# The first two modulation vectors read in units of two row blocks, scale before shift

## The chip, the cores and the metric

The kernel runs on one core of a Trainium2 chip. The metric is the device time of one execution, in microseconds (us). Five engines work side by side, each through its own queue in order: TensorE (PE: matrix products; PEld: its weight loads), VectorE (DVE), ScalarE (ACT), GpSimd (POOL) and SyncE (SP), which here issues nearly all DMA transfers.

## The reference, cut to what matters

Two decoder layers over 256 tokens of width 1024: a gated-linear-attention mixer (GLA) with a dense feed-forward, then an attention mixer with eight experts. Before each part the tokens are normalized, scaled and shifted with vectors computed from a conditioning vector `c`:

```python
cond = jax.nn.silu(c)
mod = (cond @ ada_w[i] + ada_b[i])[:, None, :]
sh1, sc1, g1, sh2, sc2, g2 = jnp.split(mod, 6, axis=-1)
h = rms_norm(x, norm_gain[i, 0]) * (1.0 + sc1) + sh1
mix = gla_mixer(h, ...)
```

`ada_w[0]` is 1024 x 6144 in float32. Its columns 0 to 1023 give the shift of the first norm and columns 1024 to 2047 its scale; with r the reciprocal root mean square of a token, h is x * r * a + s, where a is the gain times (1 + scale) and s is the shift. Only these two vectors and this first norm are touched here.

## The kernel before

All products of the first layer are split: a float32 weight tile `raw` is cast on ScalarE to a rounded high part `whi` (line 224), VectorE subtracts to get the low part `wlo` (line 226), and TensorE adds three products. The activations are split likewise into `h_gla_h` and `h_gla_l`.

Weights come in units of 1 MB into a pool of seven `raw` buffers; `unit` (line 203) issues each transfer on SP's queue, and the order of the queues is set by a scheduler at build time.

The first stage (`with wk.phase("first")`) goes like this. `ada_first` takes eight units, alternately of the scale (`j` = 1) and of the shift (`j` = 0); each has all 1024 rows and 256 columns, so the rows that the DMA moves are 1 KB long. For each unit three of the eight row blocks of 128 (`PE_K` = 3) are multiplied on TensorE (line 279, result `adar`), five on VectorE into `afa` (lines 281 and 283); one further product on TensorE adds `afa` up over the partitions (line 285), ScalarE copies the row out (line 287), two small products turn it into a column (line 291), and VectorE adds the bias and multiplies by the gain (lines 294, 296). Each unit thus finishes a quarter of one vector.

Between these, `during` issues the small transfers and the tokens `xtok` (1 MB), and ScalarE and TensorE make the sums of squares and the transposed tokens `xT`. `Norm.scale` turns the reciprocal root into a 128x256 tile `n_rs_gla` (TensorE, then a VectorE copy, line 400). `Norm.apply` then makes each of eight blocks of h: GpSimd multiplies `xT` by `n_rs_gla` (line 410), ScalarE scales and shifts into `h_gla_h` (line 411), VectorE does the same (line 412) and subtracts (line 413). As a quarter of a and s finishes, two blocks of h can be made.

Then GLA begins. Its first weights are Q (head 0's query and key columns, two transfers of 512 KB with rows of 512 B), V and R, 1 MB each. Their tiles are cast in four parts of 128x512. `qk` are Q's products, `v` and `r` those of V and R; `glow` is a narrow product for the forget gate, copied to `gT` and used by `z`. Three more vectors of ada_w (`ada_gen`, in units of two row blocks x 1024 columns, rows of 4 KB) are mixed in on VectorE (`adacc`, lines 320 and 322).

## Time and profile before

| | us |
|---|---|
| median of 3 runs | 1490.9 |
| lowest, highest | 1485.96, 1493.13 |
| the profiled execution | 1488.84 |
| its span, first to last instruction | 1487.1 |

| engine | busy us | share of the span |
|---|---|---|
| PE | 1411.8 | 95% |
| DVE | 957.3 | 64% |
| ACT | 695.2 | 47% |
| POOL | 80.4 | 5% |

The page gives each engine's busy time over the whole span, which averages stages with different limits. The span cut in 40 slices shows when TensorE was not busy; the stretch views give busy times, the granted clock (1.00 is 2.4 GHz, 0.50 is 1.2 GHz) and the DMA rate of a stage; the chain of waits says what the end was waiting for; the timeline gives single instructions with their start, length and what released them. Times in these views count from the start of the span.

### The profile page before, as it was taken

What the parts mean: (1) busy time and instruction counts of PE and PEld (TensorE: products, weight loads), DVE (VectorE), ACT (ScalarE), POOL (GpSimd) and SP (SyncE); (2) the same over time, 40 slices, a digit from 0 to 9 for tenths busy, and PEclk for the clock granted to TensorE, in tenths of its full rate; (3) what the DMA queues carried; (4) which work ended last, traced back from release to release, by engine and by line L of the source; (5) the groups of instructions that cost most, each with busy time, mean ns of one, the idle gap of its engine ahead of it and who ended that gap; (6) DMA issues with size and microseconds to landing.
All of it is one profiled execution on the core that took longest, in us unless ns stands there. A gap on an engine that the chain in (4) does not pass through costs nothing.

```text
span 1487.1 us, 21658 instructions
## 1 busy us (share of the span) xinstructions
PE 1411.8 (95%) x8443; PEld 1075.4 (72%) x8443; DVE 957.3 (64%) x1292; ACT 695.2 (47%) x984; POOL 80.4 (5%) x87
## 2 busy tenths in 40 slices
PE   6999999999999997999997999997999997999986
PEld 2899999999999997888532788532888433888422
DVE  7786897778987777799410989500989402989201
ACT  3653644335566555687300777301777202777000
POOL 2000200000132024000000000000000000000000
PEclk9999999999999998899999999999999999999998
DMA  9996578898855334699799999999999999999996
GB/s 316 362 337 221 198 267 321 302 327 286 285 169 152 132 114 170 245 348 385 281 411 403 409 408 402 393 409 402 409 408 403 393 408 403 409 406 405 380 406 261
DMA packets 183000, 488.86 MB, mean 329 GB/s; under 512 B 10815, under 2 KB 51913, under 8 KB 182890
## 3 DMA queue, kind: packets, MB, share of 16 engines
q1 hardware_dynamic: 182602, 486.87, 87.8%
q8 instruction: 68, 1.11, 0.3%
q10 hardware_dynamic: 288, 0.52, 0.1%
q14 instruction: 42, 0.34, 0.1%
HBM read 486.32 MB, written 1.05 MB: 328 GB/s over the span
## 4 chain that ended last, share of the span: by engine, by line
PE 84%; DMA 11%; DVE 3%; SPq 1%; issue 0%; ACT 0%; DVEq 0%
PE mo L1258 10%; PE mo L243 7%; PE mo L241 7%; PE mo L242 7%; DMA raw<-in_moe_w_down_dram 6%; PE md L241 4%; PE md L242 4%; PE md L243 3%; PE gu L247 3%; PE gu L249 3%; PE gu L248 3%; PE md L1258 3%; DMA raw<-in_moe_w_gate_dram 3%; PE dn L247 2%; PE dn L248 2%; PE dn L249 2%
## 5 line engine op out<-in xcount | busy, mean ns | idle before, releaser
L226 DVE TENSOR_TENSOR wlo<-raw,whi 128x1024 fp32r<-128x1024 f32 (+2 forms) x481 | 567.7, 1230 | 59.4 <-ACT whi L224 57.6
L224 ACT CAST whi<-raw 128x1024 fp32r<-128x1024 f32 (+2 forms) x491 | 486.2, 1053 | 199.6 <-PE gu L248 67.2
L1258 PE MATMUL mo<-raw,gs 128*64 128x512 f32 (+1 forms) x1024 | 205.6, 543 | 13.4 <-DMA raw<-in_moe_w_up_dram 7.2
L241 PE MATMUL mo<-whi,g 128*128 128x512 f32 x448 | 176.3, 394 | 0.9 <-ACT gf L1145 0.9
L242 PE MATMUL mo<-whi,g 128*128 128x512 f32 x448 | 175.7, 392 | 0.0
L1258 PEld LDWEIGHTS mo<-raw,gs 128*64 128x64 f32 x1024 | 70.3, 137 | 135.0 <-issue 101.2
L1301 DVE TENSOR_TENSOR msg<-msg,mo 128x512 f32<-128x512 f32 (+1 forms) x16 | 9.9, 620 | 218.8 <-PE mo L1258 218.8
L243 PE MATMUL mo<-wlo,g 128*128 128x512 f32 x448 | 148.0, 396 | 0.0
L1258 PE MATMUL md<-raw,gs 128*64 128x512 f32 x448 | 104.3, 600 | 13.6 <-DMA raw<-in_moe_w_down_dram 13.6
L241 PEld LDWEIGHTS mo<-whi,g 128*128 128x128 f32 x448 | 84.8, 189 | 19.8 <-issue 1.1
L243 PEld LDWEIGHTS mo<-wlo,g 128*128 128x128 f32 x448 | 83.7, 189 | 20.1 <-DVE wlo L226 3.5
L242 PEld LDWEIGHTS mo<-whi,g 128*128 128x128 f32 x448 | 84.8, 189 | 17.9
L322 DVE SCALAR_TENSOR_TENSOR adacc<-raw,csil,adacc 128x1024 f32<-128x1024 f32 x70 | 90.0, 1286 | 7.5 <-DMA raw<-in_ada_w_dram 7.1
L1270 ACT COPY gs<-actT 128x512 f32<-128x512 f32 (+1 forms) x16 | 8.5, 533 | 179.8 <-PE md L1258 117.8
L249 PE MATMUL gu<-h_ffn_h,wlo 128*128 128x256 f32 x320 | 90.5, 284 | 0.0
L248 PE MATMUL gu<-h_ffn_l,whi 128*128 128x256 f32 x320 | 90.1, 282 | 0.0
L247 PE MATMUL gu<-h_ffn_h,whi 128*128 128x256 f32 x320 | 89.9, 283 | 0.0
L1258 PEld LDWEIGHTS md<-raw,gs 128*64 128x64 f32 x448 | 29.2, 136 | 80.2 <-issue 48.7
L241 PE MATMUL md<-whi,act_h 128*128 128x512 f32 x192 | 76.0, 396 | 0.0
L242 PE MATMUL md<-whi,act_l 128*128 128x512 f32 x192 | 75.8, 395 | 0.0
L243 PE MATMUL md<-wlo,act_h 128*128 128x512 f32 x192 | 64.0, 400 | 0.0
L248 PE MATMUL dn<-act_l,whi 128*128 128x256 f32 x224 | 62.2, 283 | 0.0
(487 smaller groups left out, 2655.3 us busy)
## 6 DMA issues: line engine op xcount, KB each, us to landing
raw<-in_moe_w_gate_dram SPq DMA_DIRECT2D x112, 1024.0 KB, 14.1
raw<-in_moe_w_up_dram SPq DMA_DIRECT2D x112, 1024.0 KB, 13.8
raw<-in_moe_w_down_dram SPq DMA_DIRECT2D x112, 1024.0 KB, 14.0
raw<-in_ada_w_dram SPq DMA_DIRECT2D x48, 1024.0 KB, 7.0
raw<-in_fox_w_in_dram SPq DMA_DIRECT2D x16, 1024.0 KB, 6.1
raw<-in_ffn_w_gate_dram SPq DMA_DIRECT2D x14, 1024.0 KB, 5.1
raw<-in_ffn_w_up_dram SPq DMA_DIRECT2D x14, 1024.0 KB, 5.8
raw<-in_ffn_w_down_dram SPq DMA_DIRECT2D x14, 1024.0 KB, 5.0
```

What stands on the lines that cost most here:

```text
L224: nc.scalar.copy(hi[:, s], raw[:, s])
L226: (nc.gpsimd if i in pool else nc.vector).tensor_tensor(lo[:, s], raw[:, s], hi[:, s].bitcast(F32), op=ALU.subtract)
L241: nc.tensor.matmul(ps, ah, wh, start=first, stop=False)
L242: nc.tensor.matmul(ps, al, wh, start=False, stop=False)
L243: return nc.tensor.matmul(ps, ah, wl, start=False, stop=last)
L247: i = nc.tensor.matmul(ps, wh, ah, start=first, stop=False)
L248: nc.tensor.matmul(ps, wh, al, start=False, stop=False)
L249: nc.tensor.matmul(ps, wl, ah, start=False, stop=last)
L322: nc.vector.scalar_tensor_tensor(a, raw[:, kk, :], csil[:, k:k + 1], a, op0=ALU.mult, op1=ALU.add)
L1258: nc.tensor.matmul(ps[64 * i:64 * (i + 1), 0:n], a, w[:, i * n:(i + 1) * n], start=first, stop=last)
L1270: nc.scalar.copy(t, pt[:, 0:hw].rearrange("p (q i t) -> p q i t", q=n, i=2))
L1301: nc.vector.tensor_mul(sg, sg, ps[:, 0:hw])
```

## The change

`ada_first` takes its eight units in another shape and order: first the four units of the scale, then the four of the shift, each of two row blocks x 1024 columns, so that the DMA's rows are 4 KB long. Units 0 and 1 hold the row blocks that TensorE multiplies (three blocks, 2 x 512 columns each) and the first one for VectorE; units 1 to 3 hold the five blocks that VectorE accumulates in a 128x1024 tile `adacc`. TensorE's rows are copied out once and turned into columns, VectorE's tile is summed over the partitions by eight one-column products, and both are added to the bias. A vector is complete only after its last unit.

The tokens are loaded behind the scale's last unit. When the shift's first unit is done, `Norm.scale` runs and x * r * a is made for all eight blocks in a tile `ua` (GpSimd, then ScalarE in place). After the shift, ScalarE adds it to give `h_gla_h`, and one VectorE instruction per block gives `h_gla_l`, in place of two. `Norm.apply` is no longer used for this norm.

```diff
--- before.py
+++ after.py
@@ -264,36 +264,39 @@
             nc.vector.tensor_mul(m, m, gain[:, g:g + KD])
 
     def ada_first(mid):
-        js = (1, 0)
-        ps = {j: wk_ps(f"adaps_{j}") for j in js}
-        for j in js:
-            mod[0, j] = cst.tile([P, KD], F32, name=f"mod_0_{j}")
-        for u in range(4):
-            for j in js:
-                c0 = j * D + u * 256
-                raw = unit([(ada_w[0][:, c0:c0 + 256], lambda v: v)], KD)
-                rp = acc_ps(f"adar_{j}_{u}")[0:1, 0:256]
-                acc = wk.tile([P, 256], F32, tag="afa", name=f"afa_{j}_{u}")
-                for k in range(KD):
+        for j in (1, 0):
+            m = mod[0, j] = cst.tile([P, KD], F32, name=f"mod_0_{j}")
+            a = ada["p"].tile([P, D], F32, tag="adacc", name=f"adacc_0_{j}", bufs=2)
+            rp = [acc_ps(f"adar_{j}_{h}")[0:1, :] for h in range(2)]
+            ps = wk_ps(f"adat_0_{j}")
+            for u in range(4):
+                raw = unit([(ada_w[0][u * 2 * P:(u + 1) * 2 * P, j * D:(j + 1) * D], lambda v: v)], 2)
+                for kk in range(2):
+                    k = 2 * u + kk
                     if k < PE_K:
-                        nc.tensor.matmul(rp, csil[:, k:k + 1], raw[:, k, :], start=(k == 0), stop=False)
+                        for h in range(2):
+                            nc.tensor.matmul(rp[h], csil[:, k:k + 1], raw[:, kk, h * 512:(h + 1) * 512], start=(k == 0),
+                                             stop=(k == PE_K - 1))
                     elif k == PE_K:
-                        nc.vector.tensor_scalar(acc, raw[:, k, :], csil[:, k:k + 1], None, op0=ALU.mult)
+                        nc.vector.tensor_scalar(a, raw[:, kk, :], csil[:, k:k + 1], None, op0=ALU.mult)
                     else:
-                        nc.vector.scalar_tensor_tensor(acc, raw[:, k, :], csil[:, k:k + 1], acc, op0=ALU.mult,
-                                                       op1=ALU.add)
-                nc.tensor.matmul(rp, ones[:, 0:1], acc, start=False, stop=True)
-                row = wk.tile([1, 256], F32, tag="afr", name=f"afr_{j}_{u}")
-                nc.scalar.copy(row, rp)
+                        nc.vector.scalar_tensor_tensor(a, raw[:, kk, :], csil[:, k:k + 1], a, op0=ALU.mult, op1=ALU.add)
+                if u == 1:
+
+                    row = wk.tile([1, D], F32, tag="afr", name=f"afr_{j}", bufs=1)
+                    for h in range(2):
+                        nc.scalar.copy(row[:, h * 512:(h + 1) * 512], rp[h])
+                    for k in range(KD):
+                        nc.tensor.matmul(ps[:, KD + k:KD + k + 1], row[:, k * P:(k + 1) * P], ones[0:1, 0:1], start=True,
+                                         stop=True)
                 mid(u, j)
-                s = slice(2 * u, 2 * u + 2)
-                for h in range(2):
-                    nc.tensor.matmul(ps[j][:, 2 * u + h:2 * u + h + 1], row[:, h * P:(h + 1) * P], ones[0:1, 0:1],
-                                     start=True, stop=True)
-                m = mod[0, j][:, s]
-                nc.vector.tensor_add(m, ps[j][:, s], bias[:, j * KD + s.start:j * KD + s.stop])
-                if j == 1:
-                    nc.vector.tensor_mul(m, m, gain[:, s])
+                if u == 2:
+                    nc.vector.tensor_add(m, ps[:, KD:2 * KD], bias[:, j * KD:(j + 1) * KD])
+            for k in range(KD):
+                nc.tensor.matmul(ps[:, k:k + 1], a[:, k * P:(k + 1) * P], ones[:, 0:1], start=True, stop=True)
+            nc.vector.tensor_add(m, m, ps[:, 0:KD])
+            if j == 1:
+                nc.vector.tensor_mul(m, m, gain[:, 0:KD])
 
     def ada_gen(todo):
         def end(i, j, a):
@@ -1448,7 +1451,7 @@
         def during(u, j):
             if (u, j) == (0, 1):
                 load_cols()
-            if (u, j) == (1, 1):
+            if (u, j) == (3, 1):
                 for b in range(NB):
                     ld.dma_start(xtok[:, b, :], x[0, b * P:(b + 1) * P, :])
                     t = wk.tile([P, D], F32, tag="xsq", name=f"xsq_{b}", bufs=1)
@@ -1460,6 +1463,11 @@
                             nc.tensor.transpose(ps[:, k, b * P:(b + 1) * P],
                                                 xtok[:, b, (2 * q + k) * P:(2 * q + k + 1) * P], ident)
                     nc.scalar.copy(xT[:, 2 * q:2 * q + 2, :], ps)
+            if (u, j) == (0, 0):
+                n0.scale(ss0)
+                for k in range(KD):
+                    nc.gpsimd.tensor_tensor(ua[:, k, 0:T], xT[:, k, :], n0.r, op=ALU.mult)
+                    nc.scalar.activation(ua[:, k, 0:T], ua[:, k, 0:T], AF.Copy, scale=mod[0, 1][:, k:k + 1])
             if (u, j) == (1, 0):
                 load_small(glac, "wg_raw", gla_w_in[0], 3072, 16)
                 for i in range(2):
@@ -1469,12 +1477,16 @@
                 for t, v, n in ((bf_c, fox_b_f, 16), (br_c, moe_b_router, E)):
                     ld.dma_start(t, bass.AP(tensor=v.tensor, offset=v.offset, ap=[[1, n], [1, 1]]))
 
+        n0 = Norm("gla", "X", lambda: mod[0, 1], lambda: mod[0, 0])
+        ua = big.tile([P, KD, W], F32, tag="Yh", name="ua")
         ada_first(during)
-        n0 = Norm("gla", "X", lambda: mod[0, 1], lambda: mod[0, 0])
-        n0.scale(ss0)
-        h, step = n0.apply("X")
+        hh, hl = at(pair("X", "h_gla"), A_, A_, slice(0, T))
         for k in range(KD):
-            step(k)
+            sh = mod[0, 0][:, k:k + 1]
+            nc.scalar.activation(hh[:, k, :], ua[:, k, 0:T], AF.Identity, bias=sh)
+            nc.vector.scalar_tensor_tensor(hl[:, k, :], ua[:, k, 0:T], sh, hh[:, k, :].bitcast(F32), op0=ALU.add,
+                                           op1=ALU.subtract)
+        h = hh, hl
     with wk.phase("gla"):
         gen = ada_gen([(0, 2), (0, 4), (0, 3)])
         go, last = gla(h, small["wg_raw"], lambda: next(gen, None))
```

Numbers at the end of a name in the next listings tell buffers apart. On SP's queue, where the last units of ada_w stand ahead of GLA's first weights (128x8x256 is a unit in the old shape or V and R, 128x2x1024 one in the new shape, 128x8x128 half of Q, g_145 the 512 KB tile of a bias row), before:

```order
L1467 DMA wgu<-in_gla_b_gate_dram 1x512
L203 DMA raw<-in_ada_w_dram 128x8x256 x2
L1470 DMA bf_c<-in_fox_b_f_dram 16x1
L1470 DMA br_c<-in_moe_b_router_dram 8x1
L203 DMA raw<-in_ada_w_dram 128x8x256 x2
L203 DMA raw<-in_gla_w_in_dram 128x8x128 x2
L301 DMA g_145<-in_ada_b_dram 128x1024
L203 DMA raw<-in_gla_w_in_dram 128x8x256 x2
L203 DMA raw<-in_ada_w_dram 128x2x1024
```

and now:

```order
L1474 DMA wgu<-in_gla_w_gate_up_dram 16x512 x2
L1475 DMA wgu<-in_gla_b_gate_dram 1x512
L203 DMA raw<-in_ada_w_dram 128x2x1024
L1478 DMA bf_c<-in_fox_b_f_dram 16x1
L1478 DMA br_c<-in_moe_b_router_dram 8x1
L304 DMA g_145<-in_ada_b_dram 128x1024
L203 DMA raw<-in_ada_w_dram 128x2x1024
L203 DMA raw<-in_gla_w_in_dram 128x8x128 x2
L203 DMA raw<-in_gla_w_in_dram 128x8x256 x2
```

The bias tile has moved from behind Q to ahead of the last unit of the shift; V and R follow Q as before.

On VectorE, around the copy of the norm's factor, n_rs_gla (afa and adacc are the sums over row blocks, n_u and h_gla_l the norm's blocks, mod the two vectors), before:

```order
L296 TENSOR_TENSOR mod_1_154<-mod_1_154,cols 128x2
L281 TENSOR_SCALAR afa_1_257<-raw,csil 128x256
L283 SCALAR_TENSOR_TENSOR afa_1_257<-raw,csil,afa_1_257 128x256 x3
L400 COPY n_rs_gla<-n_r_gla 128x256
L283 SCALAR_TENSOR_TENSOR afa_1_257<-raw,csil,afa_1_257 128x256
L281 TENSOR_SCALAR afa_2_280<-raw,csil 128x256
L412 TENSOR_SCALAR n_u_gla_365<-n_u_gla_365,mod_1_154,mod_0_155 128x256
L283 SCALAR_TENSOR_TENSOR afa_2_280<-raw,csil,afa_2_280 128x256
L413 TENSOR_TENSOR h_gla_l<-n_u_gla_365,h_gla_h 128x256
L412 TENSOR_SCALAR n_u_gla_370<-n_u_gla_370,mod_1_154,mod_0_155 128x256
```

and now:

```order
L281 TENSOR_SCALAR adacc_0_243<-raw,csil 128x1024
L283 SCALAR_TENSOR_TENSOR adacc_0_243<-raw,csil,adacc_0_243 128x1024
L403 COPY n_rs_gla<-n_r_gla 128x256
L283 SCALAR_TENSOR_TENSOR adacc_0_243<-raw,csil,adacc_0_243 128x1024 x2
L294 TENSOR_TENSOR mod_0_242<-adat_0_246,bias 128x8
L283 SCALAR_TENSOR_TENSOR adacc_0_243<-raw,csil,adacc_0_243 128x1024
L643 MEMSET gT 33x256
L489 TENSOR_TENSOR wg<-wg_raw,wg 128x8x16
L226 TENSOR_TENSOR wlo<-raw,whi 128x512 x2
L297 TENSOR_TENSOR mod_0_242<-mod_0_242,adat_0_246 128x8
L226 TENSOR_TENSOR wlo<-raw,whi 128x512 x2
L1487 SCALAR_TENSOR_TENSOR h_gla_l<-ua,mod_0_242,h_gla_h 128x256 x8
```

The copy stood after three of the second scale quarter's five small steps; it now stands behind the shift's second 1024-wide step, the first that reads the third unit, and Q's `wlo` stand ahead of all of h_gla_l.

On ScalarE, around the casts of Q's weights (the first four casts to whi), before:

```order
L411 ACTIVATE h_gla_h<-n_u_gla_380,mod_0_155,mod_1_154 128x256
L287 COPY afr_2_290<-adar_2_279 1x256
L287 COPY afr_2_309<-adar_2_298 1x256
L411 ACTIVATE h_gla_h<-n_u_gla_385,mod_0_155,mod_1_154 128x256
L411 ACTIVATE h_gla_h<-n_u_gla_390,mod_0_155,mod_1_154 128x256
L287 COPY afr_3_329<-adar_3_318 1x256
L224 CAST whi<-raw 128x512 x4
L287 COPY afr_3_348<-adar_3_337 1x256
L224 CAST whi<-raw 128x512 x4
L411 ACTIVATE h_gla_h<-n_u_gla_395,mod_0_155,mod_1_154 128x256
L411 ACTIVATE h_gla_h<-n_u_gla_400,mod_0_155,mod_1_154 128x256
L224 CAST whi<-raw 128x512 x4
```

and now:

```order
L288 COPY afr_283<-adar_0_244 1x512
L1470 ACTIVATE ua<-ua,mod_1_154 128x256
L288 COPY afr_283<-adar_1_245 1x512
L1470 ACTIVATE ua<-ua,mod_1_154 128x256 x7
L488 CAST wg<-wg_raw 128x8x16
L224 CAST whi<-raw 128x512 x4
L1486 ACTIVATE h_gla_h<-ua,mod_0_242 128x256 x8
L224 CAST whi<-raw 128x512 x8
```

Six blocks of h_gla_h stood ahead of Q's casts and two behind V's; now eight steps on ua and the cast of wg stand ahead of Q's casts, and all of h_gla_h behind them.

## Rows read from the trace of the kernel before

**Rows 1.** page part 2, 40 slices of the span: TensorE busy tenths, DMA busy tenths

```profile
PE   6999999999999997999997999997999997999986
...
DMA  9996578898855334699799999999999999999996
```

**Rows 2.** busy time of each engine in stretches (x instructions), granted TensorE clock, DMA, GB/s

```profile
0.00:37.00 37.00, 24.55 (x113) 10.90 (x113) 28.51 (x89) 12.28 (x26) 9.82 (x22) 1.00 1.02 316
37.00:45.00 8.00, 7.62 (x44) 6.77 (x44) 4.55 (x12) 4.98 (x11) 0.00 (x0) 0.79 1.08 364
45.00:60.00 15.00, 15.00 (x127) 14.61 (x126) 14.44 (x20) 7.28 (x10) 0.57 (x2) 1.00 1.08 359
60.00:75.00 15.00, 15.00 (x102) 12.70 (x102) 11.37 (x10) 13.55 (x18) 0.00 (x0) 1.00 1.08 362
```

**Rows 3.** chain that ended last, first 120 us: start us, us, what

```profile
22.73 0.63 DVE afa L281
...
38.05 0.61 DVE wlo L226
38.71 0.63 PE qk L249 x2
...
43.34 0.53 PE adaps L291 x4
```

**Rows 4.** DMA from 20 to 31 us, the 1 KB rows

```profile
DMA packets 3915, 3.82 MB, mean 347 GB/s; under 512 B 109, under 2 KB 3915, under 8 KB 3915
```

**Rows 5.** DMA from 700 to 1400 us, the 4 KB rows of the experts

```profile
GB/s 353 348 248 408 410 394 410 408 410 408 409 395 409 408 374 410 408 399 406 409 408 409 408 402 402 409 393 390 410 408 396 409 408 409 409 409 395 409 408 347
DMA packets 78054, 277.63 MB, mean 397 GB/s; under 512 B 4226, under 2 KB 4226, under 8 KB 78012
```

**Rows 6.** timeline: start us, us, engine line op out<-in xcount [idle before <-releaser]

```profile
18.97 0.35 DVE L281 TENSOR_SCALAR afa<-raw,csil 128x256 f32<-128x256 f32 x1 [0.73 <-DMA raw<-in_ada_w_dram]
...
21.12 0.42 DVE L400 COPY n_rs_gla<-n_r_gla 128x256 f32<-128x256 f32 x1 [0.24 <-PE n_r_gla L397]
21.46 0.47 DVE L283 SCALAR_TENSOR_TENSOR afa<-raw,csil,afa 128x256 f32<-128x256 f32 x1
21.69 2.24 POOL L410 TENSOR_TENSOR n_u_gla<-xT,n_rs_gla 128x256 f32<-128x256 f32 x3 [3.89 <-DVE n_rs_gla L400]
...
22.73 0.63 DVE L281 TENSOR_SCALAR afa<-raw,csil 128x256 f32<-128x256 f32 x1 [0.79 <-DMA raw<-in_ada_w_dram]
...
25.06 0.94 DVE L283 SCALAR_TENSOR_TENSOR afa<-raw,csil,afa 128x256 f32<-128x256 f32 x1
...
25.78 1.46 PE L279 MATMUL adar<-raw,csil 128*1 128x256 f32 x6 [1.05 <-DMA raw<-in_ada_w_dram]
...
29.38 2.11 POOL L410 TENSOR_TENSOR n_u_gla<-xT,n_rs_gla 128x256 f32<-128x256 f32 x2 [2.00 <-DVE h_gla_l L413]
...
36.42 2.18 ACT L224 CAST whi<-raw 128x512 fp32r<-128x512 f32 x4 [0.36 <-DMA raw<-in_gla_w_in_dram]
...
37.09 0.38 PE L247 MATMUL qk<-h_gla_h,whi 128*128 128x256 f32 x1 [0.38 <-ACT whi L224]
```

**Rows 7.** groups of instructions, 0 to 50 us: busy us, mean ns, idle before

```profile
L283 DVE SCALAR_TENSOR_TENSOR afa<-raw,csil,afa 128x256 f32<-128x256 f32 x32 | 16.7, 523 | 0.6
...
L410 POOL TENSOR_TENSOR n_u_gla<-xT,n_rs_gla 128x256 f32<-128x256 f32 x8 | 6.8, 870 | 12.3 <-DVE h_gla_l L413 8.4 <-DVE n_rs_gla L400 3.9
...
L411 ACT ACTIVATE h_gla_h<-n_u_gla,mod,mod 128x256 fp32r<-128x256 f32 x8 | 4.5, 595 | 7.6 <-DVE mod L294 4.6 <-POOL n_u_gla L410 3.0
...
L485 ACT CAST wg<-wg_raw 128x128 fp32r<-128x128 f32 x1 | 0.3, 304 | 1.2 <-DVE h_gla_l L413 1.2
```

**Rows 8.** the same view, VectorE, 40 to 200 us

```profile
L322 DVE SCALAR_TENSOR_TENSOR adacc<-raw,csil,adacc 128x1024 f32<-128x1024 f32 x26 | 33.2, 1277 | 0.2
```

**Rows 9.** TensorE busy (x instructions), its granted clock, DMA, GB/s in stretches

```profile
39.00:42.00 3.00, 3.00 (x16) 0.50 1.11 359
...
585.00:606.00 21.00, 14.86 (x54) 0.51 0.57 214
```

## The prediction, made before the changed kernel was run

> **What bounds the kernel now.** I read the 40 slices first. TensorE is busy 9 tenths or more almost everywhere but in the first slice, and the DMA is at 9 through the first five slices [rows 1]. The edited stage lies in the first 45 us, so I went to the stretches. From 0 to 37 us TensorE is busy 24.55 us and the DMA's share is 1.02; from 45 us on TensorE is busy 15.00 us of every 15, with 127 instructions in the first such stretch, that is 0.118 us for a product of 256 columns [rows 2]. So TensorE sets the time from about 39 us on, and what the first stage is worth is read from one moment: when GLA's products first run without a gap. An earlier such moment moves all that follows, since later transfers are issued as `raw` buffers come free.
>
> The chain of waits gives the moment. It runs through a first-stage step on VectorE at 22.73 that waited for its unit, through VectorE's steps up to Q's first `wlo` at 38.05, and from 38.71 through TensorE [rows 3]. The first product of Q came at 37.09 behind a cast that had waited for Q's transfer until 36.42 [rows 6]. Four products ran before the gap that ended at 38.71 (4 x 0.118 = 0.47), and 0.53 us of the old stage's column products still came later, at 43.34 [rows 3]. The moment to compare with is therefore 38.71 - 0.47 + 0.53 = **38.8 us**. DMA and VectorE were nearly level there: Q landed at about 36.4, VectorE's last steps ended at 38.
>
> **The change part by part: the transfers.** A unit of 1.049 MB with 1 KB rows moves at 347 GB/s, 3.02 us [rows 4]; the trace has 22.73 to 25.78 between two landings [rows 6]. The experts' 4 KB rows hold 408 to 410 GB/s in most slices, 397 in the mean [rows 5]: 2.57 us a unit (2.64 by the mean). I take 2.57, since the tokens behind the scale are 4 KB rows too and nothing else shares the queue: 0.45 us saved a unit, 3.6 on eight. A unit's content is the same, so no other transfer pays.
>
> The Trainium skill, page "DMA: Bandwidth & Descriptors", section Specifications, gives 512 B as the smallest transfer at line rate, by which 1 KB rows would already be at full speed and the edit would save nothing. The rows above disagree, 347 against 408 GB/s, and I go by them; what the other reading would give is the third rival.
>
> The third unit of the shift is seventh of eight. The sixth landed at 25.78 before, so the seventh now lands at 25.78 + 3.02 - 7 x 0.45 = **25.7 us**. The bias tile (0.52 MB, 1.3 us at 408 GB/s) now goes ahead of the eighth: 25.7 + 1.3 + 2.6 = 29.6. Q, seen at 36.42, comes 3.6 earlier and 1.3 later: **34.1 us**.
>
> **VectorE's sums and the shift.** Before, the stage had 32 steps of 523 ns in `afa` [rows 7] and two norm steps a block. Now it has eight 1024-wide steps of 1.28 us [rows 8], two shorter ones, and one norm step a block. That is some 10 us less, most of which buys nothing: VectorE waits for units (idle 0.73 and 0.79 us ahead of two of them [rows 6]). What counts is the order. The copy of `n_rs_gla` stands behind the shift's second 1024-wide step, which needs the seventh unit: 25.7 + 1.28 + 0.42 for the copy [rows 6] = 27.4 us. Before, that copy was made at 21.12 [rows 6]. So all eight GpSimd products, made in pieces behind the old stage, now begin at 27.5 us, although x and its norm are there long before.
>
> **GpSimd, where I have to choose.** Three of them took 2.24 us, 0.75 each, with VectorE mostly idle [rows 6]: eight take 6.0 and end at 33.5. But three VectorE steps of 1.28 us, with two tile inputs, run in the same stretch. Where they met before, a 0.47 us VectorE step took 0.94 and GpSimd's pair took 2.11, 1.05 each [rows 6]; the mean of all eight is 870 ns [rows 7]. The upper bound is that GpSimd stands for the whole of each: 6.0 + 3 x 1.28 = 9.8, ending at 37.3. The 0.47 that VectorE's step grew by is most of one GpSimd product, so the rows lie near the upper end, and I take 36.9.
>
> The page "SBUF — State Buffer" of the Trainium skill, section "SBUF: two separate sides", says that a VectorE instruction with two SBUF inputs and a GpSimd one that reads SBUF exclude each other for a whole instruction. By that the end would be the upper bound, by the free row alone the lower; the lengthened rows agree with it in kind.
>
> **ScalarE and TensorE behind it.** ScalarE follows GpSimd with its last step on `ua` (0.60 [rows 7]), then the cast of wg (0.30), then the four casts of Q (2.18 [rows 6]), then the first `h_gla_h` (0.60). From 33.5 that gives 37.2 for the first product, from 37.3 it gives 41.0. Q's landing at 34.1 is covered in both. `h_gla_l` needs the fourth `wlo`, 0.6 behind the casts (0.61 [rows 3]), and one step of 0.5 [rows 7]: the fourth product starts 0.5 us behind the first, with 0.35 us of work between, so the moment is 37.4 to 41.2. After that ScalarE gives a block each 0.6 us, VectorE one each 0.5, and TensorE needs 8 products, 0.94 us, for it: no further gap. The shift itself is early: eighth unit 29.6, two steps and 16 one-column products, about 34 even with GpSimd's delays.
>
> So the DMA's 3.6 us are saved, and the edit puts GpSimd's eight products, ScalarE's eight and Q's casts in one row behind the seventh unit, which takes 3.6 us or more of them back. **Sum**: 37.4 - 38.8 = -1.4 at best, 41.2 - 38.8 = +2.4 at worst, taken **+2.0**.
>
> **Into GLA.** TensorE's `z` now stands behind 14 of V's products and waits for the copy of `gT`, which stands on VectorE behind eight `h_gla_l`, seven `wlo` and one 1024-wide step: 41.6 + 8 x 0.5 + 7 x 0.61 + 1.28 + 0.4 = 51.6. TensorE gets there at 41.2 + 78 x 0.118 = 50.4, with the low clock that followed its start before (0.50 for 3 us [rows 9], 1.5 us) 51.9. Cover is 0.3 us; without it V's other 34 products wait as well, for at most about 1 us. VectorE is busy 14.44 of 15 us there and 11.37 in the next stretch [rows 2], so a delay is made up. I cost it at nothing, bounds 0 and 1.
>
> Against the profiled execution's 1488.8 the sum gives 1490.8. That run lies 2.1 below the median of 1490.9, from which it would be 1492.9. I put the forecast between, **1492 us**. A measurement here tells 0.5%, 7.5 us, from no change.
>
> **The rivals.** *First, the saving arrives.* GpSimd isn't held up, so Q's products start at 37.4; or VectorE's copy comes sooner than I think because the third unit does. If the full 3.6 came through, the end would be 1488.8 - 3.6 = 1485.2; with -1.4 it is 1487.4. For it: the first three products at 0.75. Against it: ScalarE's and GpSimd's row alone takes 9.7 us from 27.5.
>
> *Second, slower, by TensorE's clock.* TensorE's work before GLA shrinks in the stretch from 27 to 41 us to 2 row blocks and some 30 small products, where before it had products every few us. At its start before, the granted clock stood at 0.50 for about 3 us [rows 9] and was 1.00 again from 45 [rows 2]. At 585 us it stood at 0.51 for 21 us [rows 9]. Were it so low here, each us would cost 0.5: 21 us cost 10.5, less the 1.5 paid already, 9.0, and with +2.0 the end is 1488.8 + 11.0 = 1499.8. It decides from 14 us of low clock on (0.5 x 14 - 1.5 + 2.0 = 7.5). Against it: once products came densely at 39 us, they got their clock back in 3 us.
>
> *Third, the new shape doesn't do what it says:* units with 4 KB rows move no faster here, so the seventh unit lands at 28.8 and everything is 3.1 us later: 1488.8 + 2.0 + 3.1 = 1493.9. Against it: 408 GB/s over 700 us [rows 5].
>
> *Fourth, the new order in GLA* makes TensorE wait for `gT` or the casts: +1 to +4 on the sum, 1492 to 1495.
>
> **How the numbers follow.** Forecast 0.47, first rival 0.20, second 0.12, third 0.06, fourth 0.15. The runs before spread over 7.2 us, so I add some 2 to 3 us at either end. From 1485 (first rival in full) to 1499 (most of the second) leaves out about 0.1 above and 0.07 below. Nearly all cases lie within 7.5 us of before: faster 0.04 (first rival with a good draw), same 0.85, slower 0.11 (most of the second, a piece of the fourth).
>
> **What would show it.** On VectorE, the copy of `n_rs_gla` near 27.4; on GpSimd, eight products from 27.5 to about 37, some of them over 1 us; on ScalarE, the first cast of Q near 38 with GpSimd or ScalarE's own row, not the DMA, as its releaser; on TensorE, the first `glow` and `qk` near 41. The DMA should show about 400 GB/s from 5 to 26 us where it had 347, and Q's landing near 34. It would be wrong if the copy comes before 25 us, if the eight products take under 7 us, if Q's cast waits for its transfer, or if the time moves while the first `qk` doesn't: then the cause lies behind 45 us, in TensorE's clock or in GLA's order.

## The result, and the profile after

The changed kernel takes 1504.0 us in the median (8 runs, 1496.8 to 1505.0), the kernel before on the same chip 1488.9 (8 runs): a ratio of 1.0091, 95% interval 1.0073 to 1.0109. That is 15 us more, outside the range of 1485 to 1499, and slower by over 0.5%, to which I had given 0.11.

The profiled execution has a span of 1503.1 us, 16.0 more than before. TensorE's granted clock over the span fell from 0.986 to 0.976. The stretches that answer to [rows 2] (columns as there: length, TensorE busy, weight loads, VectorE, ScalarE, GpSimd, granted clock, DMA share, GB/s):

```profile
0.00:37.00 37.00, 26.43 (x95) 13.23 (x95) 17.32 (x44) 10.54 (x19) 8.42 (x19) 0.84 0.97 331
37.00:45.00 8.00, 5.15 (x23) 4.77 (x24) 4.64 (x12) 6.55 (x15) 3.50 (x6) 0.50 1.09 353
45.00:60.00 15.00, 15.00 (x101) 13.25 (x100) 14.76 (x21) 10.35 (x16) 0.00 (x0) 0.88 1.07 372
60.00:75.00 15.00, 14.57 (x102) 12.77 (x101) 12.53 (x14) 12.75 (x20) 0.00 (x0) 1.00 1.08 359
```

VectorE has 11 us less work in the first 37 us, as the edit promised, and TensorE runs at half clock where it ran at full: 0.84 against 1.00 to 37 us, 0.50 against 0.79 to 45, 0.88 against 1.00 to 60. The chain of waits of the changed kernel, in the part that answers to [rows 3] (start us, us, what):

```profile
18.88 3.58 PE adat L296 x16
22.46 2.88 PE x L1463 x13
25.33 4.97 PE adar L278 x8
30.30 0.66 PE n_r_gla L400 x4
30.98 0.44 DVE n_rs_gla L403
...
35.54 4.41 POOL ua L1469 x5
...
40.38 0.28 ACT wg L488
40.67 0.53 ACT whi L224
...
44.24 0.39 PE glow L497
```

From 18.9 to 31 us TensorE itself is the chain: the scale's one-column sums, the tokens' transposes and the shift's first row blocks stand in its queue ahead of the norm's matmul. Then come GpSimd and ScalarE, in the order that I had forecast.

The 16 us sit in two places. The experts' first product with `g`, the tile of their gathered tokens, came at 599.65 us before and at 604.76 now: **5.1 us are lost by then**, all of them ahead of the dense stage, which began at 161.9 and at 167.8. From that product to the last group of `sc`, the products that scatter the experts' results back, it took 877.0 us before and 887.9 now: **10.9 us are lost in the experts**, whose instructions and whose order on each engine the edit does not touch. I had not looked there at all.

The first of these differences holds for the two executions profiled and no further. Three later profiles, of kernels with the start of the kernel before (below: routing later, new places, large tiles lower), began the dense stage at 157.7, 158.8 and 159.2. From 135 to 150 us TensorE's granted clock was 0.77 in the profile of the kernel before and 1.00 in those three. So single executions of one start differ by some 4 us, and the price of the start is better taken from medians of whole times.

At each of three places where a small expert pass ends and the next pair begins, the products now start like this (timeline: start us, us, engine line op out<-in):

```profile
825.98 0.74 PE L1202 MATMUL sc<-yh,ohT 64*128 64x512 f32 x2 [1.44 <-ACT yh L1193]
...
827.69 0.80 PE L241 MATMUL mo<-whi,g 128*128 128x512 f32 x1
828.28 0.63 PE L242 MATMUL mo<-whi,g 128*128 128x512 f32 x1
...
830.39 0.40 PE L241 MATMUL mo<-whi,g 128*128 128x512 f32 x1
```

and in the kernel before like this:

```profile
820.06 0.73 PE L1199 MATMUL sc<-yh,ohT 64*128 64x512 f32 x2 [1.44 <-ACT yh L1190]
...
821.45 0.50 PE L241 MATMUL mo<-whi,g 128*128 128x512 f32 x1
821.78 0.40 PE L242 MATMUL mo<-whi,g 128*128 128x512 f32 x1
```

The same pause of 1.44 us, the same products, but in the changed kernel the granted clock stands at 0.50 for a few us behind it, and a product takes 0.63 us instead of 0.40.

### The profile page after: what moved, and what is told of

The parts are those of the page before. It is cut to its first block, busy times and chain, and to the rows that moved or that the text cites. A ratio compares the mean times of both kernels' runs of the same rounds, so it can differ in the third digit from the quotient of the medians.

```text
span 1503.1 us, 21603 instructions
## 1 busy us (share of the span) xinstructions
PE 1425.5 (95%) x8435; PEld 1082.2 (72%) x8435; DVE 950.1 (63%) x1247; ACT 698.4 (46%) x989; POOL 84.9 (6%) x87
## 4 chain that ended last, share of the span: by engine, by line
PE 83%; DMA 11%; DVE 3%; ACT 1%; issue 1%; POOL 1%; SPq 0%; DVEq 0%; POOLq 0%
PE mo L1261 10%; PE mo L241 7%; PE mo L243 7%; PE mo L242 7%; DMA raw<-in_moe_w_down_dram 6%; PE md L241 4%; PE md L242 4%; PE md L243 3%; PE gu L247 3%; PE gu L249 3%; PE gu L248 3%; DMA raw<-in_moe_w_gate_dram 3%; PE md L1261 3%; PE dn L248 2%; PE dn L247 2%; PE dn L249 2%
## 5 line engine op out<-in xcount | busy, mean ns | idle before, releaser
L241 PE MATMUL mo<-whi,g 128*128 128x512 f32 x448 | 180.5, 403 | 0.9 <-ACT gf L1148 0.9
L242 PE MATMUL mo<-whi,g 128*128 128x512 f32 x448 | 179.0, 400 | 0.0
```

The source lines that it names most:

```text
L241: nc.tensor.matmul(ps, ah, wh, start=first, stop=False)
L242: nc.tensor.matmul(ps, al, wh, start=False, stop=False)
```

## The experiments

**What was open.** For the experts I had two theories at first: C, that the falls of the clock make all of the loss and depend on the moment alone, and D, that something in the changed program does. For the start, B: TensorE's queue, at half clock, holds the norm's copy.

**Moving the experts in time.** The kernel before with two more comparisons in the routing, and the changed kernel with one more:

```diff
             nc.vector.tensor_tensor(gt, lj, li, op=ALU.is_gt)
+            nc.vector.tensor_tensor(gt, lj, li, op=ALU.is_gt)
+            nc.vector.tensor_tensor(gt, lj, li, op=ALU.is_gt)
```

> The kernel before, with one comparison of the routing done three times instead of once, some 2.5 us more on VectorE's chain just ahead of the expert stage; nothing else is touched, and the experts' instructions are the same. Theory C (the 10 us that the change lost in the experts are the fall of TensorE's clock at the three passages from an expert's first pass to the next pair, and whether the clock falls there depends only on the moment at which the short pause of that place comes): moved by 2.4 to 3.1 us the passages of the kernel before should show the fall too, and the time goes up by the 2.5 us and by up to 10 more, to about 1498 to 1502. Rival D (the loss in the experts belongs to the changed code: other buffers, other addresses, another layout): the experts keep their times, and only the delay is added, 1490.5 to 1492.

> The changed kernel, with another comparison of the routing done twice, some 0.7 us more ahead of the experts. Theory C: a shift of 0.4 to 0.8 us takes the passages out of the falls that they show, and the time comes DOWN although work is added, to about 1494 to 1496; it stays if the shift is a little short. Rival D: 1504.0 + 0.7 = about 1504.7.

Measured: the first 1489.9 us (ratio 1.0006, 0.9989 to 1.0023), no fall; the second 1503.5 (1.0098, 1.0067 to 1.0129), all three falls. In the traces, from the first `foxo` (a product of the second layer's attention) to the first `mo`, the delays came to 1.9 and 1.3 us, not to the 2.4 to 3.1 and 0.4 to 0.8 that I had expected. Neither changed the side. C as I had put it, that it makes the whole loss, found no support, though two delays of that size, against starts that differ by some 4 us from execution to execution, could not refute it; D stayed.

**The units alone.** The changed kernel with the norm made behind both vectors again, as in the kernel before:

```diff
-            if (u, j) == (0, 0):
-                n0.scale(ss0)
...
         ada_first(during)
+        n0 = Norm("gla", "X", lambda: mod[0, 1], lambda: mod[0, 0])
+        n0.scale(ss0)
+        h, step = n0.apply("X")
```

> The changed kernel with the second part undone: units of two row blocks x 1024 columns, scale first, then shift, but the first norm made behind both, as before. Theory B (the start is late because the copy of x's norm stands behind the shift's sums in TensorE's queue, which run at half clock): the norm's matmul stands still further back there, the copy comes at some 34 us, and the first product of Q at 41.5 to 44, within 1.5 us of the changed kernel's 43.26: the units alone bring the loss of the start, and the early norm brings nothing back. Rival (the loss is the scaling ahead of the shift, its eight steps on GpSimd and eight on ScalarE): the first product returns to 37 to 39. The time with it: first product's shift against 43.26, and 0 or up to -10 from the experts.

Measured 1496.0 us (1.0058, 1.0040 to 1.0076). The first product of Q came at 40.7, between the two theories' ranges, and the dense stage began at 165.6 against 161.9 before and 167.8 after the whole change. So the units without the early norm bring a loss of their own: 6.8 us by the medians (1496.0 against 1489.1 for the kernel before beside it). And the experts took 877.7 us, as before: what slows them belongs to the other part of the edit, the early norm.

**The norm first.** TensorE's matmuls of the norm ahead of the shift's row blocks, and the copy ahead of VectorE's second step of the shift:

```diff
+                    with after(*(() if j == 1 or k == PE_K else by_r[k < PE_K])):
                         if k < PE_K:
```

> The changed kernel, with the norm's two matmuls ahead of the shift's sums in TensorE's queue and the copy of the norm ahead of the shift's second step in VectorE's. Theory B: the matmul goes at about 25.4 instead of 30.2, the copy at about 26 instead of 31.0, GpSimd's eight products end at 34 to 36 instead of 39.9, ScalarE is free for Q's casts when Q lands (35.1), and the first product of Q comes at 38.5 to 40 instead of 43.26: the stages behind move up by 3 to 4.5 us. Rival (Q's landing or the last unit's sums set the end anyway): the copy is early, and the first product moves by less than 1.5 us. The whole time: theory B 1499.5 to 1501 with the falls in the experts as they are, about 1490 if the shift takes them away.

Measured 1505.4 us (1.0120, 1.0097 to 1.0142), where theory B asked for 1499.5 to 1501. The timeline of this kernel:

```profile
25.66 0.42 DVE L406 COPY n_rs_gla<-n_r_gla 128x256 f32<-128x256 f32 x1 [1.18 <-PE n_r_gla L403]
26.23 8.45 POOL L1472 TENSOR_TENSOR ua<-xT,n_rs_gla 128x256 f32<-128x256 f32 x8 [5.73 <-DVE n_rs_gla L406]
...
35.82 2.18 ACT L224 CAST whi<-raw 128x512 fp32r<-128x512 f32 x4
35.96 1.28 DVE L286 SCALAR_TENSOR_TENSOR adacc<-raw,csil,adacc 128x1024 f32<-128x1024 f32 x1
...
37.30 3.57 PE L299 MATMUL adat<-ones,adacc 128*128 128x1 f32 x16 [1.95 <-DVE adacc L286]
...
41.10 3.30 ACT L1491 ACTIVATE h_gla_h<-ua,mod 128x256 fp32r<-128x256 f32 x8 [0.16 <-DVE mod L300]
41.71 0.39 PE L499 MATMUL glow<-h_gla_h,wg 128*32 128x256 f32 x1 [0.84 <-issue]
```

Copy, GpSimd and ScalarE moved up by some five us each, as theory B said, and the first product by 1.55 only (43.26 to 41.71). A second chain of the same length lay behind the first: the shift's own last sum. Its last step on VectorE stands behind an addition of the bias that waits for TensorE, then come eight one-column products at half clock (sixteen entries in the trace, 3.57 us), and only then can ScalarE shift. B had the first chain right and its worth wrong.

**The places of the tiles.** The experts' groups gave the lead. VectorE adds a finished half of `mo` to `msg`; between two such additions of the large pass TensorE is busy without a gap on a fixed set of products that load blocks of `g` and `act`. Before (the first fence) the stretches are 867.70 - 844.99 = 22.71 and 33.88 us, in the changed kernel (the second) 23.27 and 34.47, and VectorE's wait for `mo` grows from 0.79 to 1.10:

```profile
844.99 1.28 DVE L1344 TENSOR_TENSOR msg<-msg,mo 128x512 f32<-128x512 f32 x2 [1.97 <-PE mo L243]
867.70 1.29 DVE L1344 TENSOR_TENSOR msg<-msg,mo 128x512 f32<-128x512 f32 x2 [0.79 <-PE mo L243]
901.58 1.28 DVE L1344 TENSOR_TENSOR msg<-msg,mo 128x512 f32<-128x512 f32 x2 [0.79 <-PE mo L243]
```

```profile
852.69 1.28 DVE L1347 TENSOR_TENSOR msg<-msg,mo 128x512 f32<-128x512 f32 x2 [2.44 <-PE mo L243]
875.96 1.28 DVE L1347 TENSOR_TENSOR msg<-msg,mo 128x512 f32<-128x512 f32 x2 [1.10 <-PE mo L243]
910.43 1.29 DVE L1347 TENSOR_TENSOR msg<-msg,mo 128x512 f32<-128x512 f32 x2 [1.11 <-PE mo L243]
```

The granted clock is 1.00 in both. The expectations and theory E below call `g` the streamed tile. The rows of the products show that it is the loaded one: each block of 128x128 of `g` goes in as the weight, and 512 columns of `whi` or `wlo` stream past it. Before, then now:

```profile
L241 PEld LDWEIGHTS mo<-whi,g x448: 186/188/329, 599.6 to 1364.0; 128*128 128x128 f32 x150
L241 PE MATMUL mo<-whi,g x448: 387/389/793, 599.6 to 1364.3; 128*128 128x512 f32 x150
```

```profile
L241 PEld LDWEIGHTS mo<-whi,g x448: 187/188/330, 604.8 to 1379.6; 128*128 128x128 f32 x150
L241 PE MATMUL mo<-whi,g x448: 392/398/796, 604.8 to 1379.8; 128*128 128x512 f32 x150
```

(ns: least, median, most.) The load takes 188 ns in both, the product 389 and 398. In the profiles up to here this differs in the three kernels that ask for `ua` first and in none of the others. `ua` is the first tile to ask the pool `big` for the tag `Yh`; with that the pool hands out its five places in another order, and `g`, which uses `Xh`, moves from byte 140864 of each partition to byte 149120. Theory E: the place of this tile decides. Two experiments move the tiles of this pool and nothing else. In the changed kernel, the pair `X` goes ahead of `ua`:

```diff
+        hh, hl = at(pair("X", "h_gla"), A_, A_, slice(0, T))
         ua = big.tile([P, KD, W], F32, tag="Yh", name="ua")
```

> The changed kernel with one line moved up: the pair of tiles for the first norm's result is asked for ahead of ua, so that the pool hands out its places in the order of the kernel before (the tile g of the experts is at byte 140864 of each partition again, not at 149120). Instructions and their order stay. Theory E (the 10 us of the experts come from the place of the tiles: the products that stream g take 232 to 235 ns from start to start in the three kernels with ua asked for first, 227 ns in the three others, and the fall of the clock belongs to it): 227 ns again, no fall at the three passages, 9 to 10.5 us back, 1493 to 1495.5. Theory C (falls by moment alone): the products stay at 232 to 235 ns, or the time stays within 2 us of 1504.

In the kernel before, a tile that nothing uses asks for `Yh` first:

```diff
+        big.tile([P, KD, W], F32, tag="Yh", name="yh_first")
         n0 = Norm("gla", "X", lambda: mod[0, 1], lambda: mod[0, 0])
```

> The kernel before, with one tile asked for ahead that nothing uses, so that the pool's places come in the changed kernel's order (g at byte 149120). No instruction is added or moved. Theory E: the products that stream g take 232 to 235 ns, the passages show falls, and the time goes up by 5 (the products alone) to 10 us (with the falls), to 1494 to 1499.5. Theory C: the time of the kernel before, 1488 to 1490.5.

Measured: the changed kernel with the old places 1494.5 us (1.0041, 1.0027 to 1.0055), 5.4 above the kernel before measured beside it, where the changed kernel stood 15.1 above the one beside it: **9.7 less** by moving one line. The kernel before with the new places took 1497.2 (1.0059, 1.0036 to 1.0081), **8.1 more** by an unused tile; its profiled execution, at 1490.1, was the fastest of five, with its first `mo` at 593.8, 5.8 earlier than in the profile of the kernel before. The additions to `msg` of the first,

```profile
848.91 1.28 DVE L1347 TENSOR_TENSOR msg<-msg,mo 128x512 f32<-128x512 f32 x2 [1.95 <-PE mo L243]
871.62 1.28 DVE L1347 TENSOR_TENSOR msg<-msg,mo 128x512 f32<-128x512 f32 x2 [0.79 <-PE mo L243]
```

and of the second:

```profile
840.14 1.28 DVE L1344 TENSOR_TENSOR msg<-msg,mo 128x512 f32<-128x512 f32 x2 [2.37 <-PE mo L243]
863.43 1.28 DVE L1344 TENSOR_TENSOR msg<-msg,mo 128x512 f32<-128x512 f32 x2 [1.10 <-PE mo L243]
```

22.71 and 23.29: E holds both ways. The pool's other tiles move with `g`, but only products with `g` change their pace. From the start of one product to the next, in the median at granted clock 1.00, those with `g` and `whi` take 227 ns before and with the old places, 233 after the change and with the new places. Those that load `act`, which lies in another pool and stays, take 233 to 234 ns in all four, and pairs of those of the small passes, whose tile `gs` moves too, follow each other at 429 ns in all four. Then two more places, one to learn what about a place matters, one in the hope of a faster kernel. In the changed kernel, `Yl` too goes ahead of the pair:

```diff
         ua = big.tile([P, KD, W], F32, tag="Yh", name="ua")
+        big.tile([P, KD, W], F32, tag="Yl", name="yl_first")
```

> The changed kernel with the places moved once more: g at byte 157376, so again 64 bytes past a multiple of 128, as in the kernel before (140864), where the changed kernel has it on a multiple of 128 (149120). If the place within 128 bytes decides: 227 ns for the products that stream g, and about 1494. If it is the distance to the weights' tiles or the region (further up is slower): 233 ns or more, and 1503 to 1506.

In the kernel before, all four streamed tiles go ahead of `xT`:

```diff
+    for tag in ("Xh", "Yh", "Xl", "Yl"):
+        big.tile([P, KD, T + 2], F32, tag=tag, name="place")
     xT = big.tile([P, KD, T], F32, tag="xT", name="xT")
```

> The kernel before, with nothing but the places of the five large tiles changed: the four that TensorE streams are asked for ahead of xT and lie at bytes 132672 (the one of g and of the dense layer's act_h), 140928, 149184 and 157440, each 8 KB or more lower than in the kernel before, and xT above them. Theory E (of the places tried, g streams at 227 ns at 140864, 232 at 157376, 233 to 235 at 149120; the dense layer's tile h_ffn_h at 116.2 ns at 140864 against 117.5 at 157376): if lower is faster or equal, g stays at 227 ns or less, the gate and up products fall to 116 to 117 ns, and the time is 1485 to 1489, at or below the kernel before. Rival (the pairing with the weights' tiles decides, not the height): some product groups get slower, g at 230 ns or more, 1491 to 1496.

Measured 1502.2 us (2 runs; 1.0088, 1.0059 to 1.0118) and 1485.7 (against 1487.7 for the kernel before beside it; ratio 0.9999, 0.9983 to 1.0016). The first refutes the remainder within 128 bytes. The second runs the products with `g` as fast as before and no faster, and its whole time can't be told from the kernel before. The fourteen profiles side by side:

| kernel | byte of `g` | stretches between additions, us | falls at the three passages | first `mo` to last group of `sc`, us |
|---|---|---|---|---|
| before | 140864 | 22.71, 33.89 | 0 | 877.0 |
| before, routing later | 140864 | 22.69, 33.89 | 0 | 878.0 |
| units alone | 140864 | 22.71, 33.89 | 0 | 877.7 |
| changed, old places | 140864 | 22.71, 33.89 | 0 | 878.0 |
| start again (below) | 140864 | 22.69, 33.89 | 0 | 875.6 |
| old places, 20 products more (below) | 140864 | 22.71, 33.89 | 1 | 879.2 |
| start again, 20 products more (below) | 140864 | 22.71, 33.89 | 0 | 875.6 |
| start again, 8 products more (below) | 140864 | 22.69, 33.87 | 2 | 878.6 |
| before, large tiles lower | 132672 | 22.71, 33.89 | 2 | 878.7 |
| changed, fourth place | 157376 | 23.18, 34.38 | 0 | 883.8 |
| before, new places | 149120 | 23.29, 34.46 | 1 | 884.1 |
| changed | 149120 | 23.27, 34.47 | 3 | 887.9 |
| changed, routing later | 149120 | 23.28, 34.46 | 3 | 888.6 |
| norm first | 149120 | 23.27, 34.46 | 3 | 889.1 |

Without a fall the experts take 875.6 to 878.0 us with `g` at 140864 and 883.8 at 157376. So by estimate the place costs some 6 to 8 us of the 10.9, and the three falls the other 4 to 5 (887.9 to 889.1 against 883.8 and 884.1, with at most one fall). The falls are not tied to the place of `g`: two came at its lowest place, three in the profiles with it at 140864, none at the fourth.

**The start again.** With the old places, and all that the norm-first run had asked for: VectorE's last step of the sum ahead of the bias, ScalarE's eight shifts ahead of the cast of the second weight unit:

```diff
+                    with after(*last_k):
                         nc.vector.tensor_add(m, ps[:, KD:2 * KD], bias[:, j * KD:(j + 1) * KD])
...
+        hold(2, *done)
```

> All that the runs so far ask for: the places of the kernel before (as in the run with the pair asked for first), the norm's matmuls ahead of the shift's sums (as before), and besides VectorE's last step of the shift's sum ahead of its bias and of the gate weights, and ScalarE's eight shifts ahead of the cast of the second weight unit. Theory (in the run with the norm first, the tail of the shift's own sums and the second unit's cast held the first product at 41.9): the last step of the sum at 34 to 34.5 instead of 36.0, the sixteen one-column products end at 38.5 to 39.5, the first product of Q at 39.3 to 40.3; with the experts as in the kernel before 1489 to 1492. Rival (Q's landing at 35.1 and the half clock behind it hold the stage whatever comes first): the first product is early, but the stage ends where it did, 1493 to 1495.

Measured 1495.1 us (1.0037, 1.0021 to 1.0053), no better than the old places alone (1494.5). The first product came at 40.9, later than forecast, because the sums still ran at half clock:

```profile
36.47 3.58 PE L300 MATMUL adat<-ones,adacc 128*128 128x1 f32 x16 [0.26 <-DVE mod L298]
```

**Keeping the clock up.** Theory F: the half clock is what the start costs. TensorE multiplies row blocks that VectorE keeps, too, into a bank that nothing reads, first all five of each vector:

```diff
+                for kk in range(2):
+                    if 2 * u + kk >= PE_K:
+                        for h in range(2):
+                            nc.tensor.matmul(spare, csil[:, 0:1], raw[:, kk, h * 512:(h + 1) * 512], start=True, stop=True)
```

> The run with the pair asked for first (places of the kernel before), and TensorE multiplies, besides its own three row blocks, the five that VectorE keeps, into a bank that nothing reads: twenty products of 512 columns more, spread over the units' landings. Theory F (the units of the change leave TensorE idle between their few products, its clock falls to 0.50 from about 19 to 26 us and 36 to 46 us, and the sums, transposes and Q's first products behind it run at half speed): the first low stretch goes, the sixteen one-column products take some 1.8 us instead of 3.6, the norm's copy comes at 27 to 29 instead of 30 to 31, the first product of Q 2 to 3 us earlier (39.3 to 40.5 against 42.3), and the stages behind move up by as much: 1491 to 1493 against 1494.5. Rival (the start is bound by the transfers and by GpSimd, ScalarE and VectorE): the clock stays up, the first product moves by less than 1 us, 1494 to 1496.

> The run with the whole order of the start changed (norm first, the sum's last step ahead, the shifts ahead of the second weight unit's cast), and the same twenty products more. Theory F: the row's transposes and the sums no longer run at half clock, so the last sum ends near 37 instead of 40.1, and the first product of Q comes at 37.5 to 39 instead of 40.9; with the products at full clock from the start the stage ends some 3 us earlier, 1490 to 1492 against 1495.1. Rival (ScalarE's copies and GpSimd's products pace the tail): the first product stays at 40 to 41 and the time at 1494 to 1496.

Measured 1502.8 us (1.0098, 1.0079 to 1.0118) and 1500.7 (1.0095, 1.0076 to 1.0115), both far off. The clock stayed at 1.00 past 46 us, but I had priced a product of 512 columns by half: the trace has two entries of some 0.44 us for each. Of the first kernel:

```profile
27.17 1.84 PE L301 MATMUL adat<-ones,adacc 128*128 128x1 f32 x16
...
35.21 8.75 PE L288 MATMUL spare<-raw,csil 128*1 128x512 f32 x20
```

The added products themselves stood ahead of the last sums for 8.75 us. What these runs give is the price of the sums at full clock, 1.84 us instead of 3.58. The last run adds only what fits into the gaps:

```diff
+                    if (j, 2 * u + kk) in ((1, 3), (1, 4), (0, 4), (0, 6)):
```

> The run with the whole order of the start changed, and only four row blocks more on TensorE (two of the scale, two of the shift, eight products of 512 columns in all, into a bank that nothing reads), in the gaps that its trace shows there (15 to 18.7 us and 31.2 to 36.5 us). Theory F (half clock): it stays at full clock to the first products, the sixteen sums take 1.8 us instead of 3.6, the first product of Q comes at 38.8 to 39.8 instead of 40.9, and the first products run at 0.12 us instead of 0.21: the dense stage starts 3 to 4 us earlier (162 to 163 instead of 165.7) and the time is 1491 to 1492.5 against 1495.1. Rival (the clock falls anyway in the wait for the last sums, or the tail of the shift holds the product): low stretch and stage as in that run, 1494.5 to 1496.

Measured 1492.2 us (1.0034, 1.0021 to 1.0047). That is within theory F's range and 3.0 less than without the added work, but the two were measured apart: over the kernel before beside it this one stands 4.3 us and that one 6.1, at ratios of 1.0034 and 1.0037 whose intervals overlap. So the whole times do not show a gain. The profiles, of one execution each, show one of some 1 us: the first product of GLA at 39.72 instead of 40.84, the dense stage at 164.8 instead of 165.7. Its stretches and its timeline:

```profile
0.00:37.00 37.00, 29.81 (x124) 12.86 (x125) 18.93 (x47) 13.36 (x27) 11.40 (x24) 1.00 0.95 332
37.00:45.00 8.00, 4.88 (x25) 4.06 (x25) 7.40 (x17) 6.92 (x17) 0.00 (x0) 0.61 1.09 354
```

```profile
24.43 0.42 DVE L412 COPY n_rs_gla<-n_r_gla 128x256 f32<-128x256 f32 x1 [0.58 <-PE n_r_gla L409]
...
32.43 2.82 DVE L287 SCALAR_TENSOR_TENSOR adacc<-raw,csil,adacc 128x1024 f32<-128x1024 f32 x2 [2.21 <-DMA raw<-in_ada_w_dram]
...
35.54 1.95 PE L305 MATMUL adat<-ones,adacc 128*128 128x1 f32 x16
35.90 2.18 ACT L224 CAST whi<-raw 128x512 fp32r<-128x512 f32 x4 [1.73 <-DMA raw<-in_gla_w_in_dram]
...
39.16 3.31 ACT L1500 ACTIVATE h_gla_h<-ua,mod 128x256 fp32r<-128x256 f32 x8 [1.08 <-DVE mod L306]
```

The clock is 1.00 to 37 us, the sums take 1.95 us. The stage did not come as early as I had expected of it, 162 to 163. A stretch of half clock remains behind 38.8 us, and the first shift waits for VectorE until 39.16, which makes Q's `wlo` ahead of the last addition.

No version is measurably faster than the kernel before. The early norm with the old units was not run, so what each of the two parts of the edit costs at the start, without the other, is known for the units alone.

## Why the prediction was wrong, point by point

- **Whole time: 1492 against 1504.0.** Three terms: the places of the tiles with the falls that came along, 9.7 us (8.1 the other way), which no step of the prediction had; the start, 5.4 us by the run with the old places (1494.5 against 1489.1; 4.0 to 8.2 by its interval), for which I had +2.0; and, the other way, a base of some 1490, between my two starts, that more runs put at 1488.9. The first was decisive. The sentence that failed is the one that an earlier or later moment "moves all that follows": it took for granted that what follows keeps its own length. The experts took 887.9 us where they had taken 877.0.
- **The copy at 27.4: it came at 30.98.** I followed VectorE's queue to the third unit, which I had at 25.7 and which was seen at 27.54. The row of the copy names TensorE's `n_r_gla` as its releaser:

```profile
27.54 1.28 DVE L283 SCALAR_TENSOR_TENSOR adacc<-raw,csil,adacc 128x1024 f32<-128x1024 f32 x1 [2.89 <-DMA raw<-in_ada_w_dram]
...
30.98 0.42 DVE L403 COPY n_rs_gla<-n_r_gla 128x256 f32<-128x256 f32 x1 [2.15 <-PE n_r_gla L400]
...
31.56 8.38 POOL L1469 TENSOR_TENSOR ua<-xT,n_rs_gla 128x256 f32<-128x256 f32 x8 [10.87 <-DVE n_rs_gla L403]
```

  I had costed the sums, transposes and row blocks on TensorE as "small", without following its queue, and at the clock of before. They are the chain from 18.9 to 31, at a granted clock of 0.50 from 18 to 28 us.
- **The transfers: half right.** From 10 to 20 us the DMA moved 415 GB/s, from 20 to 35 only 329:

```profile
10.00:20.00 10.00, 8.49 (x36) 4.11 (x34) 6.32 (x11) 3.45 (x6) 0.03 (x1) 0.90 1.03 415
20.00:35.00 15.00, 14.49 (x56) 8.14 (x56) 5.61 (x7) 4.02 (x8) 4.13 (x4) 0.73 1.06 329
```

  So the 4 KB rows do what [rows 5] said, and the page of the Trainium skill that I set against it ("DMA: Bandwidth & Descriptors", section Specifications) is not borne out. But the saving was gone by the end of the stage: the issue of two small transfers held SP's queue for 9.73 us, and the last two units were issued behind it, at 20.89 and 24.36:

```profile
10.79 9.73 SPq L1474 DMA_DIRECT2D wgu<-in_gla_w_gate_up_dram  x2
...
20.89 0.39 SPq L203 DMA_DIRECT2D raw<-in_ada_w_dram  x1
...
24.36 0.39 SPq L203 DMA_DIRECT2D raw<-in_ada_w_dram  x1
```

  The last run saw Q at 35.9, where I had 34.1 and [rows 6] have 36.42. I had counted the queue's order and not the time that an issue holds it.
- **GpSimd: right.** Forecast 9.4 us for eight products between bounds of 6.0 and 9.8; measured 8.38, from 31.56 to 39.94: five of 0.71 to 0.73 us and three of 1.62 to 1.70, where VectorE's long steps lie, two of which took 1.63 and 1.77 instead of 1.28. The page "SBUF — State Buffer" of the Trainium skill, section "SBUF: two separate sides", says that GpSimd and a VectorE instruction with two inputs exclude each other for a whole instruction; the lengths agree in kind.
- **ScalarE behind it: right in kind.** wg at 40.38, Q's casts from 40.57 released by its own row and not by the DMA, first `glow` 43.26 against "near 41".
- **"The shift itself is early, about 34": wrong by 8.6 us.** Its last unit was seen at 32.4 in the last run and not at 29.6; in the changed kernel VectorE's last step stood behind an addition that waits for TensorE, the sums ran at half clock, and the addition was done at 42.6. So two chains end at 42 to 43 us, and freeing one of them buys 1.55.
- **The second rival, the clock,** was the right suspect with a wrong price. I bounded it by one long low stretch behind the start of Q, 9 us. Taking away what lay ahead of 38.8 us brought some 1 us in the profiles and nothing that the whole times can tell; part of it lay ahead of Q, where TensorE's sums and transposes are themselves on the chain. The row blocks that before came a few at a time now stand in two of every four units, and between them TensorE has little to do.
- **GLA's order: right.** `z` came at 55.2 instead of 59.8, TensorE lost 0.43 of the 15 us from 60 on, within my 0 to 1.

## What to carry to other kernels

An edit that asks a pool for one tile earlier can move the tiles that the pool hands out after it: print the places before and after, and keep the order of first use when you mean to change something else. Where a stage is short of work for TensorE, follow its queue too, at half clock, and spread the work that it has over the landings. And look for the second chain before you price the removal of the first.

## What the runs showed of the hardware

**The place of the loaded tile.** Products of 512 columns that load blocks of `g` run some 2 to 2.5% slower with `g` at bytes 149120 and 157376 than at 132672 and 140864 (23.18 to 23.29 against 22.69 to 22.71 us for the same stretch, at granted clock 1.00), in every execution profiled. The remainder within 128 bytes does not explain it, for it is 64 at 140864 and at 157376. The four places would fit a bound between 140864 and 149120, though the highest is not the slowest; the cause stays open. The page "SBUF — State Buffer" of the Trainium skill, section "SBUF: two separate sides", says that TensorE never waits on anyone among the engines; whether the slower pace is a wait, no run here shows.

**The falls of the clock.** Over the 14 profiles there are 42 passages with the same pause of 1.44 us, 15 with a fall to 0.50. The place of `g` does not decide which (table above), and the instructions do not decide alone how the clock goes: the kernel before and the one with the routing later have the same start, and from 135 to 150 us their granted clocks were 0.77 and 1.00. The page "TensorE: Matmul & The Clock Gate" of the Trainium skill, Part 1, says that the gate's window runs free and does not start with the kernel; these two executions agree with it. What makes one passage fall and the next not is not shown here. In the eight executions of the changed kernel the granted clock lies between 0.975 and 0.983, so it is likely that not all have three falls; that is argued, not shown. By estimate a fall costs some 1.5 us with `g` at 149120 (three for 4 to 5 us); at the faster places its cost can't be told from the spread of the executions without one, 875.6 to 878.0.
